# Input projections as seven block products instead of eight, in two phases per layer

## The chip, the cores and the metric

The kernel runs on one core of one Trainium2 chip. The metric is the device time of one execution in microseconds (us). Engines are named as in the profile: TensorE (PE, with its weight loads PEld), VectorE (DVE), ScalarE (ACT), GpSimd (POOL) and SyncE (SP), whose queue issues most DMAs.

## The reference, cut to what matters

Two decoder layers over 528 tokens (16 learned meta tokens and 512 real ones) of width 2048, all in float32.

- Layer 0: `h = h + concat(o_a, o_b) @ w_out`, where `proj = rmsnorm(h) @ w_in` has 8192 columns: retention q, k (1024 each), v, gate z_a (2048 each), S5 input u and gate z_b (1024 each). Retention has 8 heads (chunks of 128 tokens, a state of 128x256); S5 is a diagonal complex state-space scan of 64 groups, followed by GELU and a gated linear unit with a 1024x1024 weight.
- Layer 1: `proj` has 6144 columns (q, k 1024 each, v, z 2048 each) and 16 more for a low-rank gate code. Gated linear attention (GLA) has 4 heads (state 256x512), then the output projection and the residual.
- A final RMSNorm; the meta positions are dropped.

## The kernel before

**Three passes.** Float32 operands are split in a high part, rounded to the fast TensorE format, and a low part (the rest). A product is three passes: high by high, low tokens by high weights, high tokens by low weights.

**The stream of weights.** `panel_steps` (L137 to L169) makes one panel of 128 output features for all tokens. It loads 512 weight rows at a time (L153, 256 KB, SP's queue) into `wr`, casts them on ScalarE to `wh` (L156) and subtracts on VectorE to `wl` (L157); three buffers of each. The matmuls are all at L167: 128 weight columns against 264 tokens, twice, or against 512 tokens where the meta tokens are not needed (`tok0=META`: q, z and output projection of layer 1). An input panel has 16 k-tiles, so 96 matmuls of 264 columns, or 48 of 512. The tokens lie in SBUF as 16 pairs `xh`, `xl`.

**Order.** In layer 0 the S5 panels come first, with the S5 tables built beside them. Then each retention head's six panels (`ret_panels`) are emitted with the preceding head's mixer (`ret_mix`, `ret_fin`) called after the first and second panel; after every two heads follows an output projection over their features (`out_proj`, 16 panels). S5's scan over chunks (L557 to L560) runs on VectorE beside panels. In layer 1 each GLA head asks for its k, q, v and z panels where it needs them, and the output projection of the head before stands inside. A scheduler orders each engine's instructions by emission and by priority: `high_priority` (WPRI) puts splits and evacuations ahead. Each engine takes its instructions in order.

Of the kernel before, what the change touches and what calls it, by code (L numbers as in the profile page):

```python
# [77 lines left out]
def tile_hybrid(ctx: ExitStack, tc: tile.TileContext, d: dict, out: bass.AP, dbg=None):  # L78
# [7 lines left out]
    wpool = es(tc.tile_pool(name="wpool", bufs=3, side="left"))  # L86
    xpool = es(tc.tile_pool(name="xpool", bufs=1, side="left"))
# [19 lines left out]
    wv = cpool.tile([P, NV], F32, name="wv")  # L107

# [5 lines left out]
    rb = cpool.tile([P, L], F32, name="rb")  # L114
    zcol = cpool.tile([P, 1], F32, name="zcol")
# [18 lines left out]
    WPRI = 3000  # L134

    def panel_steps(res, wsrc, row0, col, xs, tok0=0, x0=None):
        """psum [128, 2, 512] = W[row0:, col:col+128]^T @ xs, float32 through three exact passes"""  # L137
        nk = len(xs)
        x0 = tok0 if x0 is None else x0
        at = psm.tile([P, 2, 512], F32, name="acc", tag="mm")  # L140
        if tok0 == 0:
            acc = at[:, :, :HALF]
            runs = [(acc[:, hf, :], slice(x0 + hf * HALF, x0 + (hf + 1) * HALF)) for hf in range(2)]
        else:
            acc = halves(at[:, 0, :])
            runs = [(at[:, 0, :], slice(x0, x0 + SEQ))]
        CK = 4

        def load(kc):
            with tc.high_priority(offset=WPRI):  # L150
                wr = wpool.tile([P, CK, P], F32, name="wr")
                r = row0 + kc * CK * P
                dma(wr, wsrc[r:r + CK * P, col:col + P].rearrange("(k p) m -> p k m", p=P))  # L153
                wh = wpool.tile([P, CK, P], F32R, name="wh")
                wl = wpool.tile([P, CK, P], F32R, name="wl")
                A.copy(wh, wr)  # L156
                V.tensor_tensor(wl, wr, wh.bitcast(F32), op=ALU.subtract)  # L157
            return wh, wl

        for kc in range(nk // CK):  # L160
            wh, wl = load(kc)
            for k in range(CK):
                kk = kc * CK + k
                xh, xl = xs[kk]
                for pi, (a, b) in enumerate(((wh, xh), (wh, xl), (wl, xh))):
                    for o, cols in runs:
                        PE.matmul(o, a[:, k, :], b[:, cols],  # L167
                                  start=(kk == 0 and pi == 0), stop=(kk == nk - 1 and pi == 2))
            yield  # L169
        res.append(acc)  # L170

    def panel(*a, **kw):
        res = []
        for _ in panel_steps(res, *a, **kw):
            pass
        return res[0]

    def panel_pair(a, b):
        res = [], []
        for _ in zip(panel_steps(res[0], *a), panel_steps(res[1], *b), strict=True):  # L180
            pass
        return res[0][0], res[1][0]
# [31 lines left out]
    for nm, n in vec_src:
        src = d[nm]
        if len(src.shape) == 2:
            src = src.rearrange("o n -> (o n)")
        dmab(vrows[r0:r0 + n], src.rearrange("(k p) -> k p", p=P))
        voff[nm] = r0
        r0 += n  # L220
    xt = [p0.tile([TB, D], F32, name="xt", tag="xt", bufs=6) for t in range(NB)]
    NS = 2
    with tc.high_priority(offset=10 * WPRI):
        dma(cst, d["cst"])
        for q in range(NS):
            cs_ = slice(q * (D // NS), (q + 1) * (D // NS))
            for t in range(NB):
                if t == 0:
                    dma(xt[t][0:META, cs_], d["meta"][:, cs_])
                    dma(xt[t][META:TB, cs_], d["x"][0, 0:TB - META, cs_])  # L230
                else:
                    dma(xt[t][:, cs_], d["x"][0, t * TB - META:(t + 1) * TB - META, cs_])
    dma(cst0, d["cst0"])
    pv = mx("pv")
    PE.transpose(pv[:, :KT], vrow0, ident[:KT, :KT])
    V.tensor_copy(wv0, pv[:, :KT])
    ssq = cpool.tile([TB, NB], F32, name="ssq")
    for k in range(KT):
        for hf in range(2):
            pt = mx("pt")  # L240
            for j in range(3):
                PE.transpose(pt[:, j * TB:(j + 1) * TB], xt[hf * 3 + j][:, k * P:(k + 1) * P], ident[:TB, :TB])  # L242
            sl = slice(hf * HALF, (hf + 1) * HALF)
            xh, xl = xhl[k]
            A.activation(xh[:, sl], pt[:, :HALF], AF.Copy, scale=vec("norm_ab_w", k))
            V.scalar_tensor_tensor(xl[:, sl], pt[:, :HALF], vec("norm_ab_w", k), xh.bitcast(F32)[:, sl],
                                   op0=ALU.mult, op1=ALU.subtract)
            raw = p0.tile([P, HALF], F32, name="raw", tag="raw", bufs=8)
            if hf:
# [20 lines left out]
    for hf in range(2):  # L270
        V.tensor_copy(rb[:, hf * HALF:(hf + 1) * HALF], pr[hf][:, :HALF])
# [1041 lines left out]
```

## Time and profile before

| what | value |
|---|---|
| median of 3 runs | 2177.31 us (2176.17 to 2179.82) |
| span of the profiled execution | 2173.9 us |
| TensorE busy | 2106.5 us, 97% |
| VectorE busy | 1160.2 us, 53% |
| ScalarE busy | 803.2 us, 37% |
| POOL busy | 71.7 us, 3% |

The span is the time from the first to the last instruction of one profiled execution; the runs' times are taken without the profiler and include what lies around the span. Busy times are unions over an engine's instructions; matmuls overlap, so the mean duration of one is longer than the distance from one to the next.

### The profile page before, as it was taken

The page shows a single profiled execution, that of the slowest core. Times are in us where ns is not written, and L with a number is a line of the kernel's source. Part 1 is how long each engine was busy: PE and PEld are TensorE (multiplying, and loading weights), DVE is VectorE, ACT ScalarE, POOL GpSimd, SP SyncE. Part 2 cuts the span into 40 slices and gives each one's busy share as a digit, 9 for nine tenths or more (in the row PEclk, how much of TensorE's full clock was granted, in tenths as well). Part 3 has the DMA queues.
Part 4 walks back from the last instruction along what each step waited for, and adds up shares of the span by engine and source line. Part 5 has one row for each costly group of instructions (what it writes and reads, how often), then busy time and mean ns, then how long its engine had stood idle before and what let it go on. Part 6 is the DMA issues. An engine that isn't in the chain of part 4 may idle for free.

```text
span 2173.9 us, 39751 instructions
## 1 busy us (share of the span) xinstructions
PE 2106.5 (97%) x16052; PEld 1947.0 (90%) x16052; DVE 1160.2 (53%) x2452; ACT 803.2 (37%) x1536; POOL 71.7 (3%) x110
## 2 busy tenths in 40 slices
PE   6998988999999999999999999999999999999998
PEld 5997887999999999999999998988798889889776
DVE  5886871534344433445444566545834573555376
ACT  5333422543332333234323354344325333533343
POOL 3100012000000000000000020000000000000000
PEclk9999998999999999999999999999999999999999
DMA  7855437652323222322333322223232223233232
GB/s 232 216 119 146 135 96 238 194 164 78 89 74 92 78 79 86 90 77 80 93 92 92 93 80 73 79 68 83 78 88 68 83 79 88 68 83 89 82 117 78
DMA packets 391374, 223.72 MB, mean 103 GB/s; under 512 B 45990, under 2 KB 375030, under 8 KB 391062
## 3 DMA queue, kind: packets, MB, share of 16 engines
q1 hardware_dynamic: 383062, 208.10, 34.0%
q0 software_dynamic: 8096, 13.07, 2.2%
q8 instruction: 126, 2.06, 0.4%
q14 instruction: 58, 0.48, 0.1%
q10 hardware_dynamic: 32, 0.01, 0.0%
HBM read 193.15 MB, written 27.92 MB: 102 GB/s over the span
## 4 chain that ended last, share of the span: by engine, by line
PE 81%; issue 8%; DMA 4%; DVE 3%; ACT 2%; SPq 1%; POOL 0%; ACTq 0%; DVEq 0%; POOLq 0%
PE acc L167 69%; PE last L1271 2%; PE po L1029 2%; PE pl L1152 1%; DMA x_d<-St 1%; DMA xt<-in_x_dram 1%; DVE wl L157 1%; PE pkv L1029 1%; DMA y_d<-Y 1%; PE po L767 1%; DMA wr<-in_w_out_c_dram 1%; PE po L766 1%; ACT wh L156 1%; PE pkv L758 0%; DMA wr<-in_w_in_ab_dram 0%
## 5 line engine op out<-in xcount | busy, mean ns | idle before, releaser
L156 ACT CAST wh<-wr 128x512 fp32r<-128x512 f32 x608 | 375.7, 620 | 1011.0 <-PE acc L167 872.5
L167 PE MATMUL acc<-xh,wh 128*128 128x264 f32 (+1 forms) x3200 | 734.6, 300 | 3.6 <-ACT wh L156 3.6
L167 PE MATMUL acc<-xh,wl 128*128 128x264 f32 (+1 forms) x3200 | 730.7, 299 | 7.5 <-DVE wl L157 7.5
L167 PE MATMUL acc<-xl,wh 128*128 128x264 f32 (+1 forms) x3200 | 729.3, 299 | 0.0
L157 DVE TENSOR_TENSOR wl<-wr,wh 128x512 fp32r<-128x512 f32 x608 | 417.1, 687 | 543.4 <-ACT wh L156 522.5
L167 PEld LDWEIGHTS acc<-xh,wl 128*128 128x128 f32 x3200 | 509.4, 189 | 29.4 <-DVE wl L157 12.1
L167 PEld LDWEIGHTS acc<-xh,wh 128*128 128x128 f32 x3200 | 510.9, 189 | 23.6 <-ACT wh L156 4.8
L167 PEld LDWEIGHTS acc<-xl,wh 128*128 128x128 f32 x3200 | 513.1, 189 | 19.4 <-issue 0.4
L167 PE MATMUL acc<-oh,wh 128*128 128x264 f32 x896 | 181.9, 284 | 0.5 <-DVE sz L343 0.5
L167 PE MATMUL acc<-oh,wl 128*128 128x264 f32 x896 | 181.8, 284 | 0.0
L167 PE MATMUL acc<-ol,wh 128*128 128x264 f32 x896 | 181.8, 285 | 0.0
L343 DVE TENSOR_TENSOR h<-acc,h 128x528 f32<-128x528 f32 (+1 forms) x144 | 100.9, 700 | 143.8 <-PE acc L167 143.3
L167 PEld LDWEIGHTS acc<-oh,wh 128*128 128x128 f32 x896 | 139.0, 189 | 0.7 <-issue 0.7
L167 PEld LDWEIGHTS acc<-ol,wh 128*128 128x128 f32 x896 | 138.7, 188 | 0.0
L167 PEld LDWEIGHTS acc<-oh,wl 128*128 128x128 f32 x896 | 138.7, 188 | 0.0
L343 DVE TENSOR_TENSOR vf<-acc,rb 128x528 f32<-128x528 f32 x32 | 22.6, 707 | 44.8 <-PE acc L167 44.7
L912 POOL TENSOR_TENSOR sqa<-sqa,s 128x528 f32<-128x528 f32 x13 | 17.3, 1329 | 883.8 <-ACT s L911 883.8
L1141 ACT ACTIVATE E<-E 128x512 f32<-128x512 f32 x48 | 29.7, 629 | 32.8 <-DVE E L343 32.6
L343 DVE TENSOR_TENSOR E<-b 128x256 f32<-128x256 f32 (+1 forms) x112 | 41.0, 409 | 0.0
L1152 PEld LDWEIGHTS pl<-qh,E 128*64 128x64 f32 x704 | 26.3, 137 | 12.2 <-issue 4.3
L343 DVE TENSOR_TENSOR E<-E,k 128x512 f32<-128x512 f32 (+1 forms) x56 | 36.3, 668 | 0.0
L242 PE MATMUL pt<-cst,xt 88*128 88x88 f32 x96 | 17.0, 315 | 16.8 <-DMA xt<-in_x_dram 8.9
(430 smaller groups left out, 2147.3 us busy)
## 6 DMA issues: line engine op xcount, KB each, us to landing
wr<-in_w_in_ab_dram SPq DMA_DIRECT2D x256, 256.0 KB
wr<-in_w_in_c_dram SPq DMA_DIRECT2D x192, 256.0 KB
wr<-in_w_out_ab_dram SPq DMA_DIRECT2D x96, 256.0 KB
wr<-in_w_out_c_dram SPq DMA_DIRECT2D x64, 256.0 KB
xT_d<-raw POOLq DMA_DIRECT2D x32, 132.0 KB, 3.7
h<-xT_d SPq DMA_DIRECT2D x16, 264.0 KB
k_d<-zero SPq DMA_DIRECT2D x8, 512.0 KB
ca_d<-CA SPq DMA_DIRECT2D x32, 128.0 KB
```

What stands on the lines that cost most here:

```text
L156: A.copy(wh, wr)
L157: V.tensor_tensor(wl, wr, wh.bitcast(F32), op=ALU.subtract)
L167: PE.matmul(o, a[:, k, :], b[:, cols], start=(kk == 0 and pi == 0), stop=(kk == nk - 1 and pi == 2))
L242: PE.transpose(pt[:, j * TB:(j + 1) * TB], xt[hf * 3 + j][:, k * P:(k + 1) * P], ident[:TB, :TB])
L343: V.tensor_tensor(o, a, b, op=op)
L766: PE.matmul(po[:, :RDV], st[:, c, :], vt[:, c, :], start=True, stop=False)
L767: PE.matmul(po[:, :RDV], q_[:, toks(c)], S, start=False, stop=True)
L912: (G if m < KT - 2 else V).tensor_tensor(sqa, sqa, s, op=ALU.add)
L1029: PE.matmul(o, a, b, start=(n == 0), stop=(n == len(todo) - 1))
L1141: A.activation(e, e, AF.Exp, scale=1.0 / 16)
L1152: PE.matmul(pl[r:r + 64, c * 64:(c + 1) * 64], kh[j][:, c * P + r:c * P + r + 64], qh[j][:, c * 64:(c + 1) * 64], start=(j == 0), stop=(j ...
L1271: PE.matmul(acc, a[:, cs_], b, start=(k == 0 and pi == 0), stop=(k == 3 and pi == 2))
```

## The change

**Block products.** `wino` replaces the panels of both input projections. It takes two panels (256 output features) at a time. The weights are a 2x2 grid of blocks (upper and lower half of the 2048 rows, first and second panel), the tokens too (upper and lower half of the rows, first and second 264 tokens). Seven products of block sums (8 k-tiles, 3 passes, 24 matmuls of 264 columns each) and seven additions give the four result blocks, where eight products stood before. So 168 matmuls stand in the place of 192, and every column now goes over all 528 tokens, also q and z of layer 1.

**Weights.** Four loads of 512 KB come in per pair, four block sums S are made on VectorE, and seven operands of 128x1024 are split by `hl` into `wh`, `wl` (three slots each, six raw slots `wr` while the extra pool is open). For the pairs after the second in layer 0, two of the seven splits get their low part in another way (`by_dma`): ScalarE writes the negated high part (L179) and a DMA of POOL's queue adds the raw weights onto it (L180, `accum_op`, 512 KB). Eight blocks of the last output projection of layer 0 do that also.

**Tokens.** The seven token operands (high and low, 8 tiles of 264 columns each) are made at the start, and in `finish` at the end of layer 0.

**Two phases.** All projections are written to DRAM (`pj_d`, `pk_d`) first: 32 pairs in layer 0, with one step of the S5 tables after each, and 24 in layer 1. Then mixers read them back. In layer 0 heads 0 and 1 come first, then four groups of 16 output panels by `cpair` (two panels from one 512 KB load), with two heads, or S5's output, or GELU, in each. In layer 1 the output projection of head hd-1 stands after head hd.

The diff, cut to its core (`panel_steps`, `ret_panels`, `out_proj` and the uses of `panel` go; the code for the S5 tables is the same computation in other pools):

```diff
+    BASE = {"wr": 4, "wh": 2, "wl": 2}
+    MORE = {"wr": 2, "wh": 1, "wl": 1}
+    count = {}
+    wplus = [None]
+    def wtile(tag, dt):
+        n = count.get(tag, 0)
+        count[tag] = n + 1
+        nb, ne = BASE[tag], MORE[tag] if wplus[0] is not None else 0
+        pool, bufs = (wk, nb) if n % (nb + ne) < nb else (wplus[0], ne)
+        return pool.tile([P, 8 * P], dt, name=tag, tag=tag, bufs=bufs)
+    def hl(src, by_dma=False):
+        wh, wl = wtile("wh", F32R), wtile("wl", F32R)
+        A.copy(wh, src)
+        if by_dma:
+            A.activation(wl, wh.bitcast(F32), AF.Copy, scale=-1.0)
+            dmab(wl, src, accum_op=ALU.add)
+        else:
+            tt(wl, src, wh.bitcast(F32), ALU.subtract)
+        return wh, wl
...
+    def wino(wsrc, col, wn, post, q=dma, by_dma=()):
+        with early():
+            raw = []
+            for r, c in ((0, 0), (8, 0), (0, 1), (8, 1)):
+                wr = wtile("wr", F32)
+                q(wr.rearrange("p (k m) -> p k m", k=8),
+                  wsrc[r * P:(r + 8) * P, col + c * P:col + (c + 1) * P].rearrange("(k p) m -> p k m", p=P))
+                raw.append(wr)
+            a11, a12, a21, a22 = raw
+            def comb(x, y, op):
+                s = wn.tile([P, 8 * P], F32, name="S", tag="S", bufs=3)
+                tt(s, x, y, op)
+                return s
+            w11 = hl(a11, 0 in by_dma)
+            s1 = comb(a21, a22, ALU.add)
+            w12 = hl(a12, 1 in by_dma)
+            s3 = comb(a11, a21, ALU.subtract)
+            s2 = comb(s1, a11, ALU.subtract)
+            ws1 = hl(s1)
+            ws2 = hl(s2)
+            ws3 = hl(s3)
+            s4 = comb(a12, s2, ALU.subtract)
+            ws4 = hl(s4)
+            w22 = hl(a22, 2 in by_dma)
+        z1, z2 = (psm.tile([P, 2, 512], F32, name="zx", tag="mm") for _ in range(2))
+        p1, p6, p5, p7 = z1[:, 0, :HALF], z1[:, 1, :HALF], z2[:, 0, :HALF], z2[:, 1, :HALF]
+        def mm(acc, w, o):
...
+        oa, ob = (wn.tile([P, L], F32, name="o", tag="o", bufs=4) for _ in range(2))
+        oa1, oa2, ob1, ob2 = oa[:, :HALF], oa[:, HALF:], ob[:, :HALF], ob[:, HALF:]
+        mm(p1, w11, B11)
+        with early():
+            A.copy(oa1, p1)
+        p2 = mx("p2")[:, :HALF]
...
+        with early():
+            A.copy(oa2, p5)
+        mm(p6, ws2, T2)
+        with early():
+            tt(ob1, p6, oa1, ALU.add)
+            tt(oa1, p2, oa1, ALU.add)
+            tt(oa2, oa2, ob1, ALU.add)
+        mm(p7, ws3, T3)
+        with early():
+            tt(ob2, p7, oa2, ALU.add)
+            tt(ob1, p7, ob1, ALU.add)
+        p3 = mx("p3")[:, :HALF]
+        mm(p3, ws4, B22)
+        with early():
+            tt(oa2, p3, oa2, ALU.add)
+            post(oa, col // P)
+        p4 = mx("p4")[:, :HALF]
+        mm(p4, w22, T4)
+        with early():
+            tt(ob1, p4, ob1, ALU.add)
+            post(ob, col // P + 1)
...
+    def cpair(wsrc, row0, nk, c0, c1, xs, use, tok0=0, x0=0, by_dma=False):
+        blocks = []
+        with early():
+            for kc in range(nk // 4):
+                wr = wtile("wr", F32)
...
+    kinds = [(C_Q, 2, put_raw), (C_U, 8, put_u), (C_Q + 2 * P, 6, put_raw), (C_K, 8, put_raw), (C_V, 16, put_v), (C_ZA, 16, put_z), (C_ZB, 8, put_z)]
+    n = 0
+    for c0, np_, post in kinds:
+        for j in range(0, np_, 2):
+            wino(w_in, c0 + j * P, wn, post, q=dma if n else A.dma_start, by_dma=(1, 2) if n > 1 else ())
+            wplus[0] = wpl
+            if n >= 1:
+                next(steps, None)
...
+    yhl, yts = [], []
+    for g in range(4):
+        cur, O = O, []
+        box = {}
+        for m in range(0, KT, 2):
+            if g < 3:
+                if m in (0, 8):
+                    hd = 2 * g + 2 + m // 8
+                    box[0] = hd, ret_mix(hd, *ret_load(hd))
+                elif m in (4, 12):
+                    ret_fin(box[0][0], O, *box[0][1])
+            if g == 0 and m in (2, 10):
+                scan(33 + 16 * (m // 8), 49 + 17 * (m // 8))
+            if g in (1, 2) and m % 4 == 2:
+                s5_out((g - 1) * 4 + m // 4)
+            if g == 3:
+                if m < 14:
+                    yts.append(load_y(m // 2 + 1))
+                gelu(m // 2, yts[m // 2])
...
+    for m in range(8):
+        cpair(w_out, RDV * RH + 512, 4, m, m + 8, Ob, finish, by_dma=True)
...
+    for c0, np_, post in ((D_K + 2 * P, 6, put_v1), (D_Q, 8, put_q1), (D_V, 16, put_v1), (D_Z, 16, put_z1)):
+        for j in range(0, np_, 2):
+            wino(w_in, c0 + j * P, wn, post)
...
         for j in range(2):
-            acc = panel(w_in, 0, D_K + hd * GDK + j * P, xhl)
             k_ = gt("k", "k", 2)
-            with early():
-                tt(halves(k_), acc, rbh, ALU.mult)
+            dma(k_, pk_d[D_K // P + hd * 2 + j])
```

**Order, ScalarE and POOL in the middle of layer 0's projections.** `wh_4618` and on belong to one pair: `wr` are raw weights, `S` block sums, `zx` the accumulators in PSUM, `o` the results.

```order
L177 CAST wh_4618<-wr_4610 128x1024 [waits DMAHW5_49,DVE_49,PE_49]
L177 CAST wh_4624<-wr_4612 128x1024 [waits DMAHW6_49,DVE_49,PE_49]
L179 ACTIVATE wl_4625<-wh_4624 128x1024 [waits DMASW7_49,PE_49,Activation_49]
L177 CAST wh_4633<-S_4622 128x1024 [waits PE_49]
L613 COPY CT1_4335<-pc_4593 64x256 [waits PE_49]
L613 COPY CT1_4335<-pc_4593 64x256
L613 COPY CT1_4335<-pc_4603 64x256 [waits PE_49]
L613 COPY CT1_4335<-pc_4603 64x256
L177 CAST wh_4637<-S_4631 128x1024 [waits DVE_49,PE_49]
L248 COPY o_4658<-zx_4656 128x264 [waits DMAHW0_49,PE_49]
L177 CAST wh_4641<-S_4629 128x1024 [waits PE_49,Activation_49]
L177 CAST wh_4647<-S_4645 128x1024 [waits DVE_49,PE_49,Activation_49]
```

Before, ScalarE had a cast of half the size per 512 rows, and `wl` was VectorE's alone:

```order
L156 CAST wh<-wr 128x512 [waits DMAHW3_49,DVE_49,PE_49]
L156 CAST wh<-wr 128x512 [waits DMAHW4_49,DVE_49,PE_49]
L156 CAST wh<-wr 128x512 [waits DMAHW5_49,DVE_49,PE_49]
L156 CAST wh<-wr 128x512 [waits DMAHW2_49,DVE_49,PE_49]
L672 COPY sw<-acc 64x528 [waits PE_49]
```

For two of the seven operands (here `wl_4625`) the low part has become a ScalarE instruction more and a DMA of POOL's queue behind it, whose row waits for ScalarE. POOL's queue holds nothing but these DMAs there.

**Order, TensorE at retention's mixers.** `po`, `pkv` are a head's output and state products, `pot` transposes; in the changed kernel these are the last rows of heads 0 and 1 and the first of an output projection (`acc`).

```order
L898 MATMUL po_9074<-vt_8992,st_9033 128x256
L890 MATMUL pkv_9078<-vt_8992,kw_9023 128x256
L899 MATMUL po_9074<-S_9072,q_8982 128x256
L898 MATMUL po_9082<-vt_8992,st_9033 128x256
L899 MATMUL po_9082<-S_9080,q_8982 128x256
L916 MATMUL pot_9117<-cst_69,on_9047 128x128 x4
L917 MATMUL pom2_9118<-cst_69,onm_9048 128x16
L916 MATMUL pot_9131<-cst_69,on_9047 128x128 x4
L917 MATMUL pom2_9132<-cst_69,onm_9048 128x16
L302 MATMUL acc_9814<-oh_9127,wh_9810 128x264 x2
L302 MATMUL acc_9840<-oh_9127,wh_9810 128x264 x2
L302 MATMUL acc_9814<-ol_9128,wh_9810 128x264 x2
```

Before, a head's rows stood between those of panels:

```order
L167 MATMUL acc_3346<-xh6_90,wh_3379 128x264 x2
L167 MATMUL acc_3346<-xl6_91,wh_3379 128x264 x2
L167 MATMUL acc_3346<-xh6_90,wl_3380 128x264 x2
L167 MATMUL acc_3346<-xh7_92,wh_3379 128x264
L750 MATMUL pom_3622<-vtm3_2817,stm3_2815 16x256
L756 MATMUL pkv_3625<-vtm3_2817,kwm3_2813 128x256
L766 MATMUL po_3629<-vt_3077,st_3604 128x256
L758 MATMUL pkv_3633<-vt_3077,kw_3594 128x256
L767 MATMUL po_3629<-S_3627,q_3068 128x256
L766 MATMUL po_3637<-vt_3077,st_3604 128x256
```

No row of a weight panel stands any more between the last projection and the first `acc_9814`.

**Order, TensorE at the first output projection of layer 1 in the changed kernel.** `pot` transposes the output of head 0, `pd` are the first scores of head 1, `acc` the output projection of head 0.

```order
L1255 MATMUL pot_21459<-cst_69,on_21351 128x128
L1334 MATMUL pd_21470<-q_21426,k_21422 128x128
L1334 MATMUL pd_21470<-q_21428,k_21424 128x128
L1334 MATMUL pd_21470<-q_21426,k_21422 128x128
L1334 MATMUL pd_21470<-q_21428,k_21424 128x128
L1334 MATMUL pd_21470<-q_21426,k_21422 128x128
L1334 MATMUL pd_21470<-q_21428,k_21424 128x128
L1334 MATMUL pd_21470<-q_21426,k_21422 128x128
L1334 MATMUL pd_21470<-q_21428,k_21424 128x128
L302 MATMUL acc_21950<-o__21437,wh_21946 128x512
L302 MATMUL acc_21950<-o__21438,wh_21946 128x512
L302 MATMUL acc_21950<-o__21437,wl_21947 128x512
```

All of head 0's mixer stands ahead of these rows, with no panel beside it; before, panels of q, v and z stood among them, as at retention.

## Rows read from the trace of the kernel before

**Rows 1.** The page: busy time by engine, in us.

```profile
PE 2106.5 (97%) x16052; PEld 1947.0 (90%) x16052; DVE 1160.2 (53%) x2452; ACT 803.2 (37%) x1536; POOL 71.7 (3%) x110
```

**Rows 2.** The page's costliest groups: splits and products.

```profile
L156 ACT CAST wh<-wr 128x512 fp32r<-128x512 f32 x608 | 375.7, 620 | 1011.0 <-PE acc L167 872.5
L167 PE MATMUL acc<-xh,wl 128*128 128x264 f32 (+1 forms) x3200 | 730.7, 299 | 7.5 <-DVE wl L157 7.5
L157 DVE TENSOR_TENSOR wl<-wr,wh 128x512 fp32r<-128x512 f32 x608 | 417.1, 687 | 543.4 <-ACT wh L156 522.5
```

**Rows 3.** Chain that ended last, pieces: start us, us, what.

```profile
1008.75 272.22 PE acc L167 x2242
...
1404.21 43.45 PE acc L167 x188
...
2118.78 45.08 PE last L1271 x192
```

**Rows 4.** Stretches: from:to, length, busy us, PEclk, DMA share, GB/s.

```profile
0.00:100.00 100.00, 77.35 (x574) 71.79 (x575) 70.32 (x211) 45.52 (x99) 25.69 (x53) 1.00 0.80 226
100.00:390.00 290.00, 262.43 (x2624) 246.84 (x2623) 187.94 (x497) 88.82 (x197) 26.65 (x40) 0.95 0.56 154
390.00:1281.00 891.00, 889.17 (x7195) 877.84 (x7194) 404.02 (x746) 316.04 (x596) 17.75 (x14) 1.00 0.33 94
...
1404.20:1619.00 214.80, 213.92 (x1386) 183.44 (x1385) 118.89 (x228) 84.38 (x152) 0.53 (x1) 1.00 0.29 79
...
2060.00:2173.90 113.90, 102.12 (x471) 81.35 (x469) 74.92 (x171) 41.66 (x85) 0.00 (x0) 0.98 0.30 97
```

**Rows 5.** Groups of VectorE by shape.

```profile
L343 DVE TENSOR_TENSOR h<-acc,h 128x528 f32<-128x528 f32 x96 | 67.8, 707 | 128.2 <-PE acc L167 128.1
L343 DVE TENSOR_TENSOR E<-b 128x256 f32<-128x256 f32 x96 | 35.9, 417 | 0.0
...
L560 DVE TENSOR_TENSOR St<-sc,sc 128x64 f32<-128x64 f32 x64 | 17.9, 280 | 1.8
...
L557 DVE TENSOR_TENSOR sc<-St,A 128x64 f32<-128x64 f32 x64 | 17.4, 273 | 1.8
...
L559 DVE TENSOR_TENSOR sc<-sc,St 128x64 f32<-128x64 f32 x64 | 17.2, 269 | 0.0
L558 DVE TENSOR_TENSOR sc<-St,A 128x64 f32<-128x64 f32 x64 | 16.8, 263 | 0.0
```

**Rows 6.** Groups of ScalarE by shape.

```profile
L771 ACT ACTIVATE jk<-on 128x256 f32<-128x256 f32 x32 | 13.3, 417 | 1.0
...
L1074 ACT ACT_TABLE_LOAD x8 | 10.3, 1283 | 0.1
```

**Rows 7.** The page's queues: packets, MB, share of 16 engines.

```profile
q1 hardware_dynamic: 383062, 208.10, 34.0%
q0 software_dynamic: 8096, 13.07, 2.2%
```

**Rows 8.** DMA issues: count, KB each, median us from issue to landing.

```profile
xT_d<-raw POOLq DMA_DIRECT2D x32, 132.0 KB, 3.7
...
x_d<-St POOLq DMA_DIRECT2D x16, 132.0 KB, 11.0
xs<-x_d POOLq DMA_DIRECT2D x8, 264.0 KB, 7.4
y_d<-Y POOLq DMA_DIRECT2D x8, 264.0 KB, 6.6
```

**Rows 9.** The tile xT_d: its DMAs to landing.

```profile
DMA to landing us min/median/max: 2.0/3.7/7.3
```

**Rows 10.** Three stretches of 10 us, columns as in rows 4.

```profile
160.00:170.00 10.00, 3.15 (x27) 2.93 (x25) 1.83 (x4) 0.88 (x2) 0.00 (x0) 0.77 0.89 130
170.00:180.00 10.00, 9.52 (x59) 9.16 (x60) 6.17 (x10) 3.13 (x6) 0.00 (x0) 0.72 0.56 147
180.00:190.00 10.00, 10.00 (x91) 9.32 (x90) 6.39 (x11) 4.29 (x11) 0.00 (x0) 1.00 0.56 149
```

More of the change, by code (lines that the diff above doesn't have):

```diff
@@ L134, in tile_hybrid, with ts, tt, stt @@
     WPRI = 3000
[L136 to L143, printed above, removed]
-        else:
[L145 to L182, printed above, removed]
+    def ts(o, i, s1, s2, op0, op1=None):
+        if op1 is None:
+            V.tensor_scalar(o, i, s1, None, op0=op0)
+        else:
+            V.tensor_scalar(o, i, s1, s2, op0=op0, op1=op1)
+    def tt(o, a, b, op):
+        V.tensor_tensor(o, a, b, op=op)
+    def stt(o, a, s, b, op0, op1):
+        V.scalar_tensor_tensor(o, a, s, b, op0=op0, op1=op1)
+    WPRI = 3000
     def early():
@@ L236, in tile_hybrid @@
     V.tensor_copy(wv0, pv[:, :KT])
[L237 to L249, printed above, removed]
-                V.tensor_copy(raw, pt[:, :HALF])
-            else:
-                A.copy(raw, pt[:, :HALF])
-            dmab(xT_d[k, :, sl], raw)
+    b11 = p0.tile([P, 8, HALF], F32, name="b11")
@@ new lines, in tile_hybrid @@
+    steps = s5_tables()
+    kinds = [(C_Q, 2, put_raw), (C_U, 8, put_u), (C_Q + 2 * P, 6, put_raw), (C_K, 8, put_raw), (C_V, 16, put_v), (C_ZA, 16, put_z), (C_ZB, 8, put_z)]
[6 more added lines that the diff above has]
+                next(steps, None)
+            n += 1
+    for _ in steps:
+        pass
@@ L798, in tile_hybrid @@
+    for hd in range(2):
+        ret_fin(hd, O, *ret_mix(hd, *ret_load(hd)))
+        scan(1 + 16 * hd, 17 + 16 * hd)
+    turn_x()
+    close_hx()
     for b4 in range(NP3):
         s5_load(b4)
-    steps = {4: (0, 1, 2), 5: (3, 4, 5, 6, 7)}
-    p_1 = ret_panels(1, "zkqzvv", lambda n: [s5_out(b4) for b4 in steps.get(n, ())])
-    s2_cm.__exit__(None, None, None)
-    s5a_cm.__exit__(None, None, None)
-    s5p_cm.__exit__(None, None, None)
-    if dbg is not None and "y_d" in dbg:
-        dma(dbg["y_d"], y_d[:, :, :, :])
@@ L858, in glu, with load_y @@
[L858 to L872 removed]
+    def load_y(m):
+        yt = fpool.tile([P, T, NC8], F32, name="yt", tag="yt", bufs=3)
+        for t in range(T):
+            dma(yt[:, t, :], y_d[m, t * GC:(t + 1) * GC].rearrange("h g c -> g h c"))
+        return yt
@@ L915, in tile_hybrid @@
-    out_proj(w_out, 2048 + 512, O, after=finish)
-    r1p_cm.__exit__(None, None, None)
-    if dbg is not None and dbg.get("stop") == "l0":
-        return
+            tt(sg, zs[m], sg, ALU.mult)
+            O.append(split(pool, sg, L, "O", 4))
+        cpair(d["s5_w_glu"][0], 0, 8, m0, m0 + 1, yhl, use)
+    Oa, Ob = [], []
+    for m in (0, 2):
+        glu(m, oap, Oa)
+    for m in (4, 6):
+        glu(m, obp, Ob)
+    close_r1p()
+    for m in range(0, KT, 2):
+        cpair(w_out, RDV * RH, 4, m, m + 1, Oa, add_h)
@@ new lines, in tile_hybrid @@
+    tt(wgc[:, :, 32:], wr, wgc.bitcast(F32)[:, :, :GR], ALU.subtract)
+    accg = psm.tile([P, 2, 512], F32, name="accg", tag="mm")
+    for hf, os in enumerate(((B11, B21), (B11, T1, B22))):
+        todo = [(0 if o in (B11, T1) else 8, o) for o in os]
+        for i, (k0, o) in enumerate(todo):
+            for k in range(8):
+                for pi, x in enumerate((HI[o], LO[o])):
+                    PE.matmul(accg[:GM, hf, :HALF], wgc[:, k0 + k, :], x[:, k, :],
+                              start=(i + k + pi == 0), stop=(i == len(todo) - 1 and k == 7 and pi == 1))
@@ L1057, in gate_weights, with add_h1 @@
         stack_a(wg, wr)
+    def add_h1(m, acc):
+        hv = halves(h[m])
+        with early():
+            tt(hv, acc, hv, ALU.add)
     done = None
```

1088 lines of the change are left out of this document (592 added, 496 removed).

## Prediction

> **What bounds the kernel now.** I read the busy times first: TensorE has work for 97% of the span, VectorE for about half [rows 1]. The costliest groups say who waits for whom: the casts to `wh` stand idle for 872.5 us because the buffers are still in use by matmuls, while matmuls wait 7.5 us in all for `wl` [rows 2]. So the kernel is bound by the matmuls of L167. The chain gives their true pace, since durations overlap: 272.22 us for 2242 is 0.1214 us for 264 columns, and 43.45 us for 188 is 0.2311 us for 512 [rows 3]. The stretches show where TensorE is not full: the start (22.7 us idle in 100), the S5 tables (27.6 in 290, granted clock 0.95) and the tail (11.8); in between, 891 us have 1.8 us idle, because mixers run beside panels [rows 4].
>
> Time that TensorE loses at full pace, before: layer 0 ends near 1281; it loses 52.1 us idle plus 14.5 by the clock in its first 390 us, and I add 16 (estimate) for matmuls that wait while their rows count as busy: 83. Layer 1 has 892.9 us. Its matmuls are 2304 x 0.1214 + 1728 x 0.2311 + 45.1 for the last projection = 724. A GLA head's period of 214.8 us holds 576 x 0.1214 + 480 x 0.2311 = 180.9 of panels, so its mixer takes 33.9 of TensorE, four of them 136; 33 us remain. Together 116 us lost.
>
> **The change, part by part.**
>
> *Matmuls.* Before, the input projections are 64 panels and 24 (k, v) of 96 matmuls, 8448 x 0.1214 = 1025.6 us, and 24 panels (q, z of layer 1) of 48 long ones, 1152 x 0.2311 = 266.2. After, 56 pairs x 168 = 9408 x 0.1214 = 1142.1. That takes 149.7 us off the path. Nothing else on TensorE changes much.
>
> *VectorE and ScalarE beside a pair (20.4 us of TensorE).* From 417 ns for 256 elements and 687 for 512 [rows 2, 5] a 128x1024 VectorE instruction is 1.23 us. A layer-1 pair has 4 sums and 7 subtractions (13.5), 7 additions of 264 at 0.43 and 2 scalings at 0.7: 17.9 us. A layer-0 pair has two subtractions less, 15.5, plus its step of the S5 tables, up to 20.2 by the sum of the rows in the order. A cast is 1.03 us (417 ns for 256 columns, 620 for 512 [rows 2, 6]), seven of them 7.2. So both fit under 20.4, VectorE narrowly; these edits I cost at nothing, hidden by the pair's matmuls.
>
> *The accumulating DMA* is the new wait on the path, 60 times. A slot of `wl` comes free when the product three earlier ends; the new part is wanted two products later, 2 x 24 x 0.1214 = 5.83 us, plus 0.24 for two passes that don't need it. Into that must go the cast (1.03), the negation (1.03), about 0.2 of hand-overs and the landing L. Above L = 3.8 us TensorE stalls by L - 3.8, 60 times. Behind the waiting cast ScalarE holds the next casts and the copies out of PSUM; POOL's queue holds only the next such DMA, SP's the raw load that wants the slot. L isn't in the trace at 512 KB. The queues move 13.07 MB in 2.2% and 208.10 MB in 34.0% of the span, some 275 GB/s with all engines [rows 7], so 512 KB is 1.9 us and 132 KB 0.5. `xT_d`, 132 KB on the same queue, lands in 3.7 us, at best 2.0 [rows 8, 9]: scaled, 3.4 to 5.1. `y_d`, 264 KB, has 6.6: scaled 7.6. The slowest, `x_d`, 11.0, would be 12.4. So the stall is 0 (L = 3.4), 78 (5.1), 228 (7.6) or 516 us (12.4). I take 0: 32 `xT_d` transfers stood behind each other in a stretch with DMA share 0.80 [rows 4], whereas these come singly, and their low end is the nearer case. The Trainium skill, "DMA: Bandwidth & Descriptors", on the anatomy of a software-queue DMA, gives about 2.0 us and bytes at 436 GB/s: by it 512 KB would be 3.2 us (an estimate) and there would be no stall; for 132 KB it would say 2.3, and the trace's median of 3.7 is longer, so the rows decide.
>
> *What loses its cover.* The time TensorE loses after, by stage:
> - Start: 26 operand instructions of 128x1056 (1.26 us, 32.8) in the place of 32 short ones, 13.5 for the first pair's weights, some 20 of scalings and additions, 12 of input DMA: the second pair starts near 78 us. Of these 20.4 (first pair) and 9 (transposes) are work: 49 lost (45 to 53), and 8 (6 to 10) in the pairs that follow.
> - Retention heads 0 and 1 have no panel beside them. The order puts 254 VectorE instructions there, about 78 us by the rows; 128 are scan steps of 0.27 [rows 5], 34.7 us. TensorE has 14: 64 lost (62 to 66).
> - The four groups, GLU, both S5 output projections and `finish`: VectorE has 48 to 78 us a group against TensorE's 47 to 61, ScalarE 6.6 a `finish` pair against 5.8: 22 (16 to 24). Start of layer 1: 7 (6 to 8).
> - GLA head 0 has nothing beside it. Of the 118.9 us that VectorE has in a head's period [rows 4], 64 subtractions (44.0), 12 evacuations (8.4) and 16 residual additions (11.0) go; 55.5 remain. ScalarE keeps 84.4 - 64 x 0.62 = 44.7, with table loads of 1.28 among them [rows 6]. Alternating, they take between 84 and 100; I take 92, less 33.9: 58 (50 to 66). Heads 1 and 2 have VectorE 76 against TensorE 78: 20 for both (10 to 30).
> - Tail as before: 12 (11 to 12).
>
> Sum 240 (206 to 269).
>
> **Sum.** 2173.9 - 149.7 + 240 - 116 = 2148 us of span; the runs' median lies 3.4 above the span, so 2151.6, 1.2% less. With the ends of the losses, 2118 to 2181.
>
> **Rivals.**
> 1. *Slower: the accumulating DMAs set the pace.* From L = 4.2 the whole gain is gone (60 x 0.43 = 26). At 5.1 the time is 2230, at 7.6 it is 2380. For it: every other row of that queue is over 3.4 [rows 8], and loads and sums keep the engines some 0.6 busy here. Against: those rows come in bunches.
> 2. *The bare mixers cost all of it.* At 269 lost the time is 2181, no change. The clock speaks for more: after 6.9 us idle in ten, the next ten had it at 0.72 of full speed (levels 1.2 and 2.4 GHz) [rows 10]. The 48 us of TensorE work in bare heads would take up to 48 us more at the low level, if all were on the path: 2200 to 2229. Against: VectorE ends those waits. The Trainium skill, "TensorE: Matmul & The Clock Gate", Part 1, has the clock halved after idling, and the rows agree (0.72).
> 3. *VectorE becomes the bound of the projections.* The S5 steps add up to 4 us over 20.4 in some 12 pairs: +48, 2200. Against: 20.2 is the largest sum I find, and rows overlap.
> 4. *Better cover.* If the scheduler brings scans, loads and first scores forward under the last pairs, half of 64 and 58 goes: 2090.
>
> **How the numbers follow.** A measurement of this kernel tells 0.2% (4.4 us) from no change. Chances: forecast (2118 to 2172) 0.45; better cover 0.11; rival 1 0.22; rival 2 0.17, half of it within 0.2%; rival 3 0.05. Faster 0.56, same 0.08, slower 0.36. The range from 2075 to 2285 leaves out the worst of rival 1. The forecast's own range is 2118 to 2181.
>
> **What would show it.** Matmuls of L242 at 0.121 us and 20.4 us a pair say the gain is there; idle on TensorE before third-pass products, put down to the POOL queue, says rival 1, with the landing time beside L180. A gap near 64 us after the last pair and near 58 in GLA head 0 bear out the losses; the clock there decides rival 2. VectorE near full between 100 and 650 us would be rival 3. I am wrong if the pair's period is not 20.4 us or if the bare heads last longer than their VectorE rows.

## The result, and the profile after

The changed kernel takes 2390.46 us (median, 2387.40 to 2395.49) against 2177.22 before: a ratio of 1.098 [1.0958, 1.1006]. It is slower by 213 us, where 1.2% less was forecast. The profiled execution has a span of 2393.7 us.

The page of the changed kernel, lines that answer to [rows 1, 2, 7, 8]: busy time by engine; matmuls of the products kept in `p` (second, sixth and seventh in order of TensorE) with the low weights; POOL's DMA queue; the accumulating DMAs with their median landing.

```profile
PE 2072.0 (87%) x15956; PEld 1932.8 (81%) x15956; DVE 1699.6 (71%) x2914; ACT 1027.1 (43%) x1606; POOL 103.4 (4%) x125
...
L242 PE MATMUL p<-bh,wl 128*128 128x264 f32 x1344 | 396.0, 295 | 89.7 <-DMA wl<-wr 89.5
...
q0 software_dynamic: 15424, 42.20, 9.0%
...
wl<-wr POOLq DMA_DIRECT2D x68, 512.0 KB, 6.2
```

TensorE's share falls from 97% to 87%, although its work became less. A part of the reason stands in the releaser of the second line: 89.5 of its 322 us of idle time end with a DMA onto `wl`, a wait that did not exist. The median landing of these DMAs is 6.2 us.

Stretches of the changed kernel (columns as in [rows 4]): start; layer 0's projections; the two bare retention heads; output projections with six heads, GLU and the first S5 output projection; `finish` and the start of layer 1; layer 1's projections; GLA head 0; heads 1 and 2; head 3 and the last projection.

```profile
0.00:93.00 93.00, 40.35 (x202) 34.91 (x203) 57.73 (x86) 37.29 (x55) 0.20 (x4) 0.76 0.39 99
93.00:888.00 795.00, 704.38 (x5753) 684.99 (x5753) 538.18 (x759) 353.95 (x453) 51.48 (x62) 0.97 0.65 165
888.00:966.00 78.00, 38.76 (x158) 30.82 (x157) 65.22 (x258) 21.75 (x63) 0.00 (x0) 0.65 0.54 173
966.00:1363.00 397.00, 367.82 (x3063) 347.90 (x3062) 227.79 (x482) 143.88 (x298) 21.62 (x32) 0.94 0.52 154
1363.00:1458.00 95.00, 72.78 (x534) 70.27 (x532) 68.61 (x118) 55.90 (x102) 27.96 (x23) 0.89 0.63 158
1458.00:1958.00 500.00, 499.52 (x4106) 499.11 (x4107) 408.64 (x491) 198.43 (x232) 0.00 (x0) 1.00 0.43 121
1958.00:2063.00 105.00, 54.44 (x374) 43.46 (x374) 69.94 (x162) 57.21 (x106) 1.05 (x2) 0.61 0.35 117
2063.00:2239.00 176.00, 159.05 (x1042) 121.93 (x1040) 153.48 (x318) 96.90 (x177) 1.05 (x2) 0.95 0.27 86
2239.00:2393.70 154.70, 134.87 (x737) 99.41 (x736) 110.00 (x246) 61.79 (x124) 0.00 (x0) 0.93 0.25 83
```

Only the layer-1 projections (1458 to 1958) look as the kernel before did between 390 and 1281 us: 0.5 us idle in 500, clock 1.00. Everywhere else TensorE waits, and where it is busy for about half of the time or less, the granted clock is low too (0.61 to 0.76).

The chain of the changed kernel in layer 1's projections, two pieces that stand one pair apart:

```profile
1702.00 8.73 PE zx L242 x72
...
1722.37 8.73 PE zx L242 x72
```

The pair's period is 20.37 us, as forecast (20.4). In layer 0's projections the chain reads otherwise. Ahead of the DMA, ScalarE has its cast and the negation as soon as a product ends; then come the landing of 4.69 us and TensorE's products:

```profile
498.61 1.05 ACT L177 CAST wh<-wr 128x1024 fp32r<-128x1024 f32 x1 [1.53 <-PE zx L242]
499.69 1.06 ACT L179 ACTIVATE wl<-wh 128x1024 fp32r<-128x1024 f32 x1
```

```profile
501.05 4.69 DMA wl<-wr
...
505.78 2.82 PE p L242 x21
```

POOL's DMAs there come 24.4 us apart from pair to pair, with the second 5.8 us behind the first:

```profile
501.05 0.85 POOL L180 DMA_DIRECT2D wl<-wr  x1 [21.37 <-ACT wl L179]
506.84 0.85 POOL L180 DMA_DIRECT2D wl<-wr  x1 [4.94 <-ACT wl L179]
525.49 0.85 POOL L180 DMA_DIRECT2D wl<-wr  x1 [17.81 <-ACT wl L179]
531.28 0.85 POOL L180 DMA_DIRECT2D wl<-wr  x1 [4.94 <-ACT wl L179]
```

TensorE stands still for both, once ahead of the seventh product and once ahead of the next pair's second:

```profile
505.78 0.39 PE L242 MATMUL p<-bh,wl 128*128 128x264 f32 x1 [1.05 <-DMA wl<-wr]
...
514.40 0.39 PE L242 MATMUL p<-bh,wl 128*128 128x264 f32 x1 [1.76 <-DMA wl<-wr]
```

The median of 6.2 hides two groups. Read one by one in layer 0's projections, the first of the two (the seventh operand) lands in 4.8 us (median; 4.69 at 501), the second (the next pair's second operand), issued right behind two raw loads of 512 KB (503.91 and 505.75), in 7.5 (7.52 at 507). In the pair shown they don't overlap: the first has landed at 505.74, the second is issued at 506.84.

### The profile page after: what moved, and what is told of

Same layout as the page of the kernel before. It is cut to its first block, busy times and chain, and to the rows that moved or that the text cites. A ratio compares the mean times of both kernels' runs of the same rounds, so it can differ in the third digit from the quotient of the medians.

```text
span 2393.7 us, 40173 instructions
## 1 busy us (share of the span) xinstructions
PE 2072.0 (87%) x15956; PEld 1932.8 (81%) x15956; DVE 1699.6 (71%) x2914; ACT 1027.1 (43%) x1606; POOL 103.4 (4%) x125
## 4 chain that ended last, share of the span: by engine, by line
PE 53%; issue 16%; DMA 14%; DVE 11%; ACT 4%; SPq 1%; ACTq 0%; POOLq 0%; DVEq 0%; POOL 0%
PE zx L242 14%; PE acc L302 14%; PE p L242 13%; DMA wl<-wr 7%; DVE wl L144 2%; PE last L1492 2%; PE po L1248 2%; PE pl L1373 1%; DMA wr<-in_w_in_ab_dram 1%; DVE sc L144 1%; DMA vf<-pj_d 1%; ACT wh L177 1%; PE pkv L1248 1%; DMA xt<-in_x_dram 1%; DMA wr<-in_w_out_c_dram 1%
## 5 line engine op out<-in xcount | busy, mean ns | idle before, releaser
L242 PE MATMUL zx<-bh,wh 128*128 128x264 f32 x1792 | 519.6, 290 | 28.1 <-ACT bh L199 14.9
L242 PE MATMUL zx<-bl,wh 128*128 128x264 f32 x1792 | 514.4, 287 | 3.9 <-DVE bl L144 3.9
L242 PE MATMUL zx<-bh,wl 128*128 128x264 f32 x1792 | 512.9, 286 | 1.4 <-DVE wl L144 1.4
L242 PE MATMUL p<-bh,wl 128*128 128x264 f32 x1344 | 396.0, 295 | 89.7 <-DMA wl<-wr 89.5
L242 PE MATMUL p<-bh,wh 128*128 128x264 f32 x1344 | 390.5, 291 | 0.7 <-ACT wh L177 0.7
L242 PE MATMUL p<-bl,wh 128*128 128x264 f32 x1344 | 388.9, 289 | 0.0
L144 DVE TENSOR_TENSOR wl<-S,wh 128x1024 fp32r<-128x1024 f32 x224 | 273.5, 1221 | 137.4 <-ACT wh L177 135.5
L242 PEld LDWEIGHTS zx<-bh,wh 128*128 128x128 f32 x1792 | 343.6, 192 | 32.1 <-ACT bh L199 15.7
L242 PEld LDWEIGHTS zx<-bl,wh 128*128 128x128 f32 x1792 | 343.5, 192 | 4.8 <-DVE bl L144 4.7
L242 PEld LDWEIGHTS zx<-bh,wl 128*128 128x128 f32 x1792 | 341.3, 190 | 2.0 <-DVE wl L144 2.0
```

What stands on the lines that cost most here:

```text
L144: V.tensor_tensor(o, a, b, op=op)
L242: PE.matmul(acc, a[:, k, :], b, start=(k == 0 and pi == 0), stop=(k == 7 and pi == 2))
```

## The experiments

Ratios are to the kernel before, on the same chip and in the same rounds; a difference between two kernels is that of their medians.

**Without the accumulating DMAs.**

```diff
-by_dma=(1, 2) if n > 1 else ()
+by_dma=()
-cpair(w_out, RDV * RH + 512, 4, m, m + 8, Ob, finish, by_dma=True)
+cpair(w_out, RDV * RH + 512, 4, m, m + 8, Ob, finish)
```

> No accumulating DMA: VectorE makes all low parts. Theory D (the DMA's landing of 6.2 us against 3.8 allowed stalls TensorE 2.46 us, 60 times in layer 0's pairs, and some 28 us in the 8 finishing blocks): the pair period of layer 0 falls from 25.3 to 20.4-21.5 us, about 2225 (2210 to 2245). Theory V (VectorE is the real limit of these pairs and the DMA wait only stands in its place): the period stays over 23.5 us, 2330 or more.

Measured: 2284.15, ratio 1.0505 [1.0485, 1.0525], 106 us less. The projections of layer 0 in this kernel:

```profile
93.00:779.00 686.00, 675.09 (x5747) 665.23 (x5745) 600.79 (x815) 291.24 (x393) 0.41 (x2) 0.99 0.51 146
```

They end at 779 us and not 888, and TensorE idles 11 us and not 91. The chain there, twice two pieces a pair apart, while S5's tables are made and behind them:

```profile
405.19 0.87 PE pc L610 x8
406.06 2.91 PE zx L242 x24
...
427.25 2.91 PE zx L242 x24
...
697.53 2.90 PE zx L242 x24
...
717.83 2.90 PE zx L242 x24
```

A pair takes 21.2 us, then 20.3; the difference is 0.87 us of TensorE's own matmuls for the tables (`pc`). So VectorE carries the seven low parts (601 us busy in 686) without setting the pace of these pairs; theory V falls. Theory D has the period right, but its 2225 us was 59 too low: it took 2.46 us for each of 60 stalls, and the trace has 89.5 us in all. The finishing blocks gained 4 us (80 with the DMAs, 76 without), which theory D had at 28: there the DMA was not the limit.

**One accumulating DMA in a pair.**

```diff
-by_dma=(1, 2) if n > 1 else ()
+by_dma=(1,) if n > 1 else ()
```

> Only the second operand's low part by DMA, the seventh's by VectorE; the finishing blocks as they were. Theory D: half of the pairs' stall goes, period 22.8 us, about 2320 (2310 to 2330). Theory V: no gain or a loss, 2390 or more, since VectorE has 1.2 us more in each pair.

Measured: 2323.06, 1.0683 [1.0655, 1.0710], 67 us less. The landing falls to 5.1 us (median), though raw loads are still there; when they come beside it was not followed. From here to none is 39 us, of which some 4 lie in the finishing blocks, whose DMAs stayed; the prediction's formula gives 30 x (5.1 - 3.8) = 39 for the pairs.

**The same bytes in two DMAs.**

```diff
-            dmab(wl, src, accum_op=ALU.add)
+            for hf in (slice(0, 4 * P), slice(4 * P, 8 * P)):
+                dmab(wl[:, hf], src[:, hf], accum_op=ALU.add)
```

> Each accumulating DMA is issued as two of 256 KB, for the first and the last four k-tiles; the matmuls of a tile wait for their own half alone. If the landing time is mostly moved bytes, the first half lands in about 3.6 us and the stall goes: 2245 (2230 to 2270). If it is mostly a fixed cost and queueing, the first half takes 5 us or more: 2310 to 2390.

Measured: 2358.20, 1.0832 [1.0801, 1.0864], 32 us less. A half lands in 5.6 us (median in layer 0's projections, where the whole has 6.3). The two halves are issued right behind each other, so this is not the price of 256 KB alone.

**A plain copy in the place of the addition.** The low parts then hold the raw weights; the subtraction is left out.

```diff
-            dmab(wl, src, accum_op=ALU.add)
+            dmab(wl, src.bitcast(F32R))
```

> The changed kernel, but the 68 DMAs copy the raw weights onto the low part instead of adding them, so the low parts are wrong; bytes, queue and waits stay. If the addition makes the DMA long (theory A): landing falls from 6.2 to 4.5 us or less and the time by 70 to 100 us, 2290 to 2320. If size and queueing do (theory C): landing stays at 5.7 or more, 2370 to 2395.

Measured: 2314.83, 1.0645 [1.0613, 1.0677], 76 us less. The landing of the DMAs onto `wl`, first of the changed kernel, then of this one:

```profile
DMA to landing us min/median/max: 4.5/6.2/9.7
```

```profile
DMA to landing us min/median/max: 2.8/4.4/8.7
```

The best case falls by 1.7 us and the median by 1.8, with the same bytes, queue and loads: the addition costs that.

**No weight loads beside the DMAs.** From the third pair on, the blocks of the second are used again.

```diff
+    kept = []
...
-            raw = []
-            for r, c in ((0, 0), (8, 0), (0, 1), (8, 1)):
+            raw = list(kept) if by_dma else []
+            for r, c in () if by_dma else ((0, 0), (8, 0), (0, 1), (8, 1)):
...
+            kept[:] = raw
```

> The changed kernel, but from the third pair of layer 0 on no raw weights are loaded, the four blocks of the second pair are used again (wrong weights); the accumulating DMAs stay and have the 16 engines nearly to themselves. If the weight loads beside them stretch them (theory C, contention): landing 4.0 to 4.6 us, 60 stalls mostly gone, 2290 to 2320. If the DMA is that slow by itself (theory A): landing 5.5 or more, 2360 to 2395.

Measured: 2326.33, 1.0696 [1.0677, 1.0714], 64 us less.

```profile
DMA to landing us min/median/max: 4.5/4.6/8.6
```

Best and median meet at 4.5 to 4.6 us: an accumulating DMA of 512 KB takes 4.5 us nearly alone, and the loads of the weights beside it add 1.6 to the median, most of it on the second of the two (7.5 to 5.0; the first 4.8 to 4.5). So both theories hold in part: 1.7 us from the addition, 1.6 from contention, and neither alone brings the landing under 3.8.

**Four slots for the low and high parts, four for raw weights.**

```diff
-    MORE = {"wr": 2, "wh": 1, "wl": 1}
+    MORE = {"wr": 0, "wh": 2, "wl": 2}
```

> The changed kernel, accumulating DMAs and all, with four slots for the high and the low parts in the place of three, and four for the raw weights in the place of six. By the prediction's step (a slot comes free two products before its use, 5.83 us) a third product adds 2.91 us, so a landing of 6.2 us is allowed: the stall goes and the time falls by 70 to 109, 2284 to 2320, if raw weights come in time. If they don't: raw loads take the stall's place, 2350 or more, with waits for the weight loads in the trace. If the slots were not the limit: 2385 to 2395.

Measured: 2374.45, 1.0915 [1.0899, 1.0931], 16 us less. TensorE's waits for DMAs onto `wl` fall to 5.6 us in layer 0's projections, but TensorE is idle there as long as before (91 us in 795). It now waits for VectorE's low parts, and the chain has gained pieces for the raw loads:

```profile
PE zx L242 <- DVE wl L144: 38.0, 15, 3.3
...
PE p L242 <- DMA wl<-wr: 5.6, 8, 1.2
```

```profile
499.69 7.65 DMA wr<-in_w_in_ab_dram
...
543.46 5.90 DMA wl<-wr
...
549.40 6.71 DMA wr<-in_w_in_ab_dram
```

The stall went where the slots were taken from. Six raw slots beside four of the others were not tried.

**An eighth product put back (without the DMAs).** Its 24 matmuls run in each pair; the result isn't used.

```diff
+        p8 = mx("p8")[:, :HALF]
+        mm(p8, w11, B11)
```

> The kernel without accumulating DMAs (2284), with an eighth product's 24 matmuls put back in each of the 56 pairs (its result isn't used). If the 149.7 us that seven products save are really on the path, all 56 x 24 x 0.1214 = 163 us come back: 2440 to 2450, layer-1 pairs at 23.3 us. If VectorE or ScalarE set a part of the pairs' period, less: 2410 or under.

Measured: 2438.66, 1.1216 [1.1195, 1.1236], 154.5 us more than without it, of 163. The chain of layer 1's projections, one pair apart:

```profile
1608.46 5.81 PE p L242 x48
...
1631.73 5.80 PE p L242 x48
```

The period is 23.27 us, 2.90 more. Matmuls of these pairs are on the path, nearly all of them; the forecast gain of 149.7 us was real, and other losses ate it.

**Without the scan (in the changed kernel).** 4 of the 64 steps of S5's scan over chunks remain; the others are left out.

```diff
-        for c in range(lo, min(hi, NC8 - 1)):
+        for c in range(lo, min(hi, lo + 1)):
```

> Leaves out nearly all steps of S5's scan over chunks (5 of 64 remain), 64 us of VectorE, half of it beside the two bare retention heads. If VectorE sets the end of that stretch, as the prediction has it: 30 to 40 us less there and 5 to 15 in the group behind, about 2350 (2340 to 2360). If latencies between engines set it (each small wait of TensorE, ScalarE and the loads from DRAM), 15 us or less in all: 2378 or more.

Measured: 2374.70, 1.0913 [1.0891, 1.0935], 16 us less. The first output product starts at 931.0 us, as with the scan (931.3); 21 us are gained behind it. So VectorE's row sum alone does not set the bare stretch. What TensorE waits for there, in the changed kernel (us in total, times, longest):

```profile
PE pvt L843 <- DMA vf<-pj_d: 18.7, 2, 16.6
PE pot L916 <- DVE on L139: 6.0, 1, 6.0
PE pom L882 <- DVE stm L144: 2.6, 1, 2.6
```

**The scan's states loaded later (without the DMAs).**

```diff
-    dma(St, st_d)
...
-        ret_fin(hd, O, *ret_mix(hd, *ret_load(hd)))
+        loaded = ret_load(hd)
+        if hd == 0:
+            dma(St, st_d)
+        ret_fin(hd, O, *ret_mix(hd, *loaded))
```

> The kernel without accumulating DMAs (2284), with the load of S5's states (2.1 MB) and so the scan behind head 0's loads. If the loads from DRAM at the change of phase set the bare stretch, as its waits say (18.7 us for v): 8 to 14 us less, 2270 to 2276. If VectorE's work sets it: 2280 to 2288.

Measured: 2282.10, 1.0496 [1.0476, 1.0517]: no difference to 2284.15 that can be told. The first output product starts 11 us earlier (813.2), and that is given back behind it.

**Neither the scan nor the early load (without the DMAs).** The edits of the two runs above together, the load behind head 0's mixer.

> The kernel without accumulating DMAs (2284), without the scan's steps (left out: S5's state between chunks) and with the load of its states late. Each alone gave nearly nothing in the bare stretch (0 and 11 us). If both are limits of about the same height there: first output projection 20 to 30 us earlier and kept, 2240 to 2255. If a third (the chain through a head: transposes, decays, norms) sets it: 2260 to 2270, as without the scan alone.

Measured: 2269.70, 1.0428 [1.0412, 1.0444], 14 us less, as without the scan alone; the first output product starts at 810.0 and not 824.3. TensorE still waits in the bare stretch of this kernel:

```profile
PE pvt L842 <- DMA vf<-pj_d: 27.0, 4, 10.5
PE pot L915 <- DVE on L139: 5.1, 1, 5.1
```

**One buffer more for those loads, and the states late (on the kernel of the squares, below).** The same edit stands at `vf` and `of`, and the states' load is moved behind head 0's loads.

```diff
-        sw = r0a.tile([P, L], F32, name="sw", tag="vf", bufs=3)
+        sw = r0a.tile([P, L], F32, name="sw", tag="vf", bufs=4)
```

> The kernel of the run before (2264), with four buffers in the place of three for the values read back from DRAM in retention's heads, and the scan's states loaded behind head 0's values. Without scan and states TensorE still waited 27 us for v there. If the loads' buffers set the bare stretch: that wait falls under 10 us and the time by 8 to 15 us, 2249 to 2256. If the chain through a head (rotation, decay, transposes, norms) sets it: within 4 us.

Measured: 2261.97, 1.0406 [1.0389, 1.0424], against 2263.60: within the noise. The wait for v falls from 21.8 to 11.5 us, those for the norms and decays stay near 17, and the median does not move. More buffers were not tried.

**Matmuls of no use beside GLA head 0 (without the DMAs).** 72 of them, `glow` against itself, behind the gates and the levels (a helper `warm`).

> The kernel without accumulating DMAs (2284), with 72 matmuls of no use beside GLA head 0, so that TensorE idles less there. If the low granted clock (0.61 over 105 us) lengthens that stretch (theory K): clock there over 0.8, stretch 90 to 97 us, 2269 to 2276. If VectorE and ScalarE alone set its length (theory V): clock up, stretch 103 to 108 us, 2280 to 2290.

Measured: 2289.23, 1.0531 [1.0510, 1.0552]. Inconclusive: they all ran between 1865 and 1888 us, ahead of the levels, and the stretch's clock stayed at 0.63. The next run ties them to each level:

```diff
+            if hd == 0:
+                at = psm.tile([P, 2, 512], F32, name="warm", tag="mm")
+                for i in range(4):
+                    PE.matmul(at[:64, 0, :256], kh[i % 2][:, :64], qh[i % 2], start=True, stop=True)
```

> The kernel without accumulating DMAs (2284), with four matmuls of no use behind each of the six score levels of GLA head 0, on that level's own operands, so that they can't be pulled forward as the 72 of the run before were. If the low granted clock lengthens that stretch: clock of the levels over 0.8, the level period falls from 4.15 us to 3.2-3.6, stretch 99 to 102 us. If VectorE sets the levels' period: period 4.0 or more, stretch 104 us or more.

Measured: 2285.62, 1.0505 [1.0486, 1.0525]: no gain. The levels' stretch without and with them (columns as before):

```profile
1880.00:1925.00 45.00, 23.75 (x241) 19.04 (x242) 36.57 (x88) 21.48 (x47) 0.53 (x1) 0.54 0.18 58
```

```profile
1880.00:1925.00 45.00, 31.71 (x297) 21.55 (x298) 37.01 (x86) 19.61 (x42) 0.53 (x1) 0.80 0.13 38
```

The clock rises from 0.54 to 0.80, and the way from the last projection product to the first output product is 102.1 us in the place of 103.2. So VectorE sets this stretch, as its waits in the changed kernel say (below). The low clock costs about 1 us here, unless the added matmuls took back what the clock gave, which this run can't tell apart.

**The tokens ahead of the first weights (without the DMAs).**

```diff
-q=dma if n else A.dma_start
+q=dma
```

> The kernel without accumulating DMAs (2284), with the first pair's weights on SP's queue among the tokens and not ahead of them on ScalarE's. If the tokens' arrival sets the start: the steady run of products begins 6 to 12 us before 93, 2272 to 2278. If VectorE's and ScalarE's splits set it: within 3 us.

Measured: 2278.06, 1.0468 [1.0452, 1.0484], 6 us less; the second product (`p`) begins at 81.7 us and not 91.8.

**The squares' sums on VectorE (with the tokens first).**

```diff
-            G.tensor_tensor(sqa, sqa, s, op=ALU.add)
+            V.tensor_tensor(sqa, sqa, s, op=ALU.add)
```

> The kernel with the tokens first (2278), with the 15 sums of squares of the finishing blocks on VectorE in the place of GpSimd. The trace has VectorE instructions of 0.49 us at 1.55 while a GpSimd addition runs, some 1.07 each. If GpSimd's additions hold VectorE up there: 15 x 1.07 = 16 us of it go and 15 x 0.7 = 10.5 come, no long instructions are left, 2270 to 2276. If the long ones have another cause: 15 x 0.7 more on a full VectorE, 2284 to 2289.

Measured: 2263.60, 1.0420 [1.0397, 1.0443], 14 us less, though VectorE, nearly full there (20.0 us busy in the last 21), has 10.5 us more to do; the expectation had 2 to 8. One split of `finish` with the sums on GpSimd, min/median/max ns, then with them on VectorE:

```profile
L147 DVE SCALAR_TENSOR_TENSOR bl<-h,wv,bh x16: 480/490/1557, 1267.2 to 1327.5; 128x264 fp32r<-128x264 f32 x16
```

```profile
L147 DVE SCALAR_TENSOR_TENSOR bl<-h,wv,bh x16: 479/489/495, 1260.1 to 1312.6; 128x264 fp32r<-128x264 f32 x16
```

No long ones are left.

## Why the prediction was wrong, step by step

Of the 239 us between forecast (2151.6) and measurement, 106 go with the accumulating DMAs, and 133 stay without them. They belong to two steps.

**The step that failed first: "I take 0".** The prediction had the mechanism (a slot of `wl` comes free two products ahead, 3.8 us are left for the landing, 60 stalls of L - 3.8), its bounds for L (3.4 to 12.4) and the case on the slow side as rival 1. It then chose the low end, by the argument that `xT_d` transfers stood behind each other and these come singly. Measured, L is 6.2: 4.5 for the transfer alone, of which 1.7 are the addition, for which no row of before had a price, and 1.6 for the weight loads, of which the prediction had said that they keep the engines some 0.6 busy (0.65 in the trace) without putting a price on it. By its own formula 6.2 gives 144 us; taking the DMAs away gives 106, and TensorE's waits put down to them are 89.5 in layer 0's projections and 8.1 in the finishing blocks. The formula has too much because it counts 60 stalls apart, each with 3.8 us of room. In the pair shown, counted by the starts of the matmuls, the first DMA is needed 3.5 us behind its issue, and TensorE loses 1.2. The second is needed 5.65 us behind its issue: its room holds the 1.2 that TensorE has just lost and 0.7 of matmuls for S5's tables. So 7.5 us of landing cost 1.9 there and not 3.7. With smaller landings the formula comes nearer (against the kernel without DMAs: 39 for 39 us with one a pair, 48 for 42 without loads, 36 for 31 with the copy; some 4 us of each measured one lie in the finishing blocks). The Trainium skill's price ("DMA: Bandwidth & Descriptors", anatomy of a software-queue DMA), 3.2 us as an estimate, would have said the same wrong thing. The trace of the plain copy has 2.8 at best and 4.4 in the median, that of the accumulating DMA 4.5 and 6.2.

**The gain was right.** 149.7 us forecast; the pair's period is 20.37 us, and an eighth product costs 154.5 of 163 us when put back. Rival 3 (VectorE as the bound of the projections) did not come: with all low parts on VectorE the pairs take 20.3 us, or 21.2 with 0.87 of TensorE's own matmuls for the tables.

**The second step that failed: "Sum 240 (206 to 269)" for the time lost without cover.** Without the DMAs the profiled execution's span is still 141 us over the sum (133 by the medians), outside these ends. By stretch of that kernel, against the lengths in the prediction's working:
- The start: 93 us with about 21 of TensorE work done (some 100 matmuls of the first pair and the transposes, an estimate from the instruction count), 72 lost where 57 were forecast (start and the pairs behind). The first weights stood ahead of the tokens, worth 6 us.
- Heads 0 and 1, the groups, GLU and the first S5 output projection: 475 us against about 438 (an estimate by the prediction's terms: 2304 weight matmuls, eight heads of 7, some 16 for S5's small products, and the 64 and 22 lost). The bare stretch is not VectorE's row sum: the scan's 35 us of it were no limit, nor the states' load, nor both together in full. By the waits, loads of v through three shared buffers and the norm and decay chain seem to stand at about the same height, so that each that is taken away uncovers the next. Which mix costs the 37 us stays open.
- `finish` and the start of layer 1: 96 us against about 62. The prediction named ScalarE (6.6 us a pair); VectorE is the limit (80.8 us busy against ScalarE's 48.9), held up by GpSimd. Moving the sums gave 14 of the 34.
- GLA head 0: 105 us against 92, over the upper end of 100 with its loads. In it TensorE waits for VectorE:

```profile
PE px L1294 <- DVE wg L144: 16.1, 1, 16.1
PE pl L1373 <- DVE E L144: 11.7, 7, 2.1
PE p L1339 <- DVE qo L144: 8.7, 2, 7.5
```

- Heads 1 and 2: 176 against 177. Head 3 and the end: 158 against about 135.

These make some 120 of the 141; where the rest lies was not followed.

**Rival 2** had the right sign and the wrong price and cause: uncovered mixers cost more than forecast, but in GLA head 0 not by the clock. The clock was low where the prediction said (0.61 there), and raising it from 0.54 to 0.80 in that head's levels took 1 us off. In the two bare retention heads (0.65) no run tells what the clock costs.

**Rival 4** (better cover) did not come: the first output product of layer 0 starts 46 us behind the last pair without the DMAs, but until the `finish` blocks TensorE is busy for only 398 of 475 us.

No version tried beats the kernel before: the best, 2262 us, is 4.1% slower. It has the gain of seven products and has lost the cover that interleaved panels gave the mixers.

## What to carry to other kernels

Fewer matmuls are worth their time only while TensorE stays the bound in every stretch, so price what the new form puts beside them and what it uncovers, stretch by stretch. Where a needed operand passes through a DMA that a slot ring holds back, the budget is the ring's lead time, and the landing is to be priced by the middle of the nearest rows and not their best (here 5.1 to 7.6 against a measured 6.2), with the traffic that the change itself adds. A stretch that was never bare can have several limits of one height, as the two retention heads here; the row sum of one engine is its lower end.

## What the runs showed of the hardware

A DMA of POOL's queue that adds 512 KB onto SBUF lands in 4.5 us at best, one that copies them in 2.8. Beside weight loads the medians are 6.2 and 4.4; without them the adding one has 4.6, and the copy was not measured without them.

GpSimd's additions and VectorE hold each other up. The timeline of the kernel without the DMAs, in `finish` (start us, us): one GpSimd addition of usual length, then one that takes 2.18 us while VectorE goes on, and behind it a VectorE split that takes 1.55 us where it else takes 0.49:

```profile
1292.51 1.33 POOL L1044 TENSOR_TENSOR sqa<-sqa,s 128x528 f32<-128x528 f32 x1 [2.13 <-ACT s L1043]
...
1296.72 2.18 POOL L1044 TENSOR_TENSOR sqa<-sqa,s 128x528 f32<-128x528 f32 x1 [2.88 <-ACT s L1043]
...
1296.95 0.42 DVE L144 TENSOR_TENSOR bl<-x,bh 128x264 fp32r<-128x264 f32 x1
...
1297.30 0.42 DVE L144 TENSOR_TENSOR bl<-t,bh 128x264 fp32r<-128x264 f32 x1
...
1297.64 1.55 DVE L147 SCALAR_TENSOR_TENSOR bl<-h,wv,bh 128x264 fp32r<-128x264 f32 x1
```

The Trainium skill ("SBUF — State Buffer", who interferes with whom, and its summary) says that a VectorE instruction with two SBUF inputs and a GpSimd instruction that reads SBUF contend for a shared port, and that the second one blocks until the first has finished. The trace agrees: the addition is 0.85 us longer than usual while two VectorE subtractions keep their 0.42, the split behind them is 1.06 longer than its 0.49, and the splits' maximum goes from 1557 to 495 ns when GpSimd's sums are gone. Before, 13 such additions of 1.33 us stood beside a VectorE that had time to spare (28.2 us busy in 39), and TensorE was busy for all of the 39.
